# A sixth buffer for raw weight chunks in the two FFNs of a hybrid decoder layer

## Chip, cores and metric

One core of one Trainium2 chip runs the whole layer in one launch. The metric is the device time of one execution in microseconds (us), the median of several runs. The kernel before the change takes 1099.44 us (three runs, 1098.82 to 1101.89).

## The reference

One decoder layer over 512 tokens of width 1024, all in float32:

```python
D_MODEL, SEQ, D_FF = 1024, 512, 2816

def swiglu_ffn(x, g, w_gate, w_up, w_down):
    h = rms_norm(x, g)
    return (jax.nn.silu(h @ w_gate) * (h @ w_up)) @ w_down

x = x + 0.5 * swiglu_ffn(x, ffn1_norm, ffn1_w_gate, ffn1_w_up, ffn1_w_down)
h = rms_norm(x, mix_norm)
... = split_columns(h @ w_in)          # two attention branches, gates
x = x + merged @ w_out                 # the mixing stage
x = x + 0.5 * swiglu_ffn(x, ffn2_norm, ffn2_w_gate, ffn2_w_up, ffn2_w_down)
```

The change lies in the two FFNs. The mixing stage between them (a forgetting attention, a sparse attention with top-k keys, gates and an output projection) stays as it is.

## The kernel before

**Arithmetic.** Every float32 operand of a matrix product is split in two parts, high (rounded to the fast format F32R) and low (what the rounding left). A product is three matmuls: high by high, low by high, high by low (`mm3`, lines 141 to 143). Activations and weights are both split. For weights `split_w` does it: ScalarE casts the raw chunk to `wh` (line 112), and VectorE subtracts `wh` from the raw chunk to get `wl` (line 117). A few chunks have their low part made by a DMA that adds the raw chunk to minus `wh` (lines 114 and 115, issued from GpSimd). `wh` and `wl` have three buffers each.

**The FFN.** The 2816 hidden features are 22 blocks of 128. They are worked through in four groups (blocks 0 to 3, 4 to 9, 10 to 15, 16 to 21). In the first group each block is two plain steps, gate and up, each with one weight chunk of 128 x 1024 numbers (512 KB). In the other groups the blocks go in pairs, three pairs to a group, with a scheme of seven products of half size where a plain computation has eight (the code calls them A, S1, S2, B, S3, S4, D, and each is a step). A pair reads four raw chunks of 512 KB, called a, b, c and d, and forms from them with VectorE three running sums s1 = c + d (line 342), s2 = s1 + a (347), c = c + a (351) and later s2 = s2 + b (355). Products collect in PSUM banks pA, pB, pC and pD. The bank pB is used three times: for S2 and S3, then read by VectorE into `gu` (line 385), then for D. Each group ends with eight down steps, one chunk each, that add to x (line 421).

**The order of the work.** TensorE's order is written out by hand: the list `steps`. The other engines' instructions are placed by the framework's planner. It lays out the queue of each engine once, when the program is built, from a simulated timeline and the order of the code, and it may pull ready work ahead. On the chip every queue is worked through in order, SyncE's, which issues the loads, among them.

**Raw buffers.** A raw chunk sits in a buffer of 128 x 1024 numbers. The names `ra`, `rb` and `rc` belong to the kernel's weight pool and serve the mixing stage too. `re` belongs to each FFN's own pool. `rd` does as well, but holds a temporary (`xn`) during the plain steps and joins the others when the pairs begin. So five buffers serve the pairs. `load` (inside `ffn`, around line 460) takes the next chunk off a list and puts it in the free name that was used longest ago; a name never used comes first. `look_ahead(i)` is called before step i: it splits the weights of steps i to i + 2, loads what these need, marks the buffers free whose last reader it has written, and then loads for up to step i + 6 as long as a name is free. Buffers c and a of a pair are marked free with step S3, b with S4, d with D. A load's DMA waits on the chip until the last reader of the buffer's former content is through. While a pair runs, it holds four buffers, and one is left for the next pair.

Of the kernel before, what the change touches and what calls it, by code (L numbers as in the profile page):

```python
# [11 lines left out]
F32 = mybir.dt.float32  # L12
# [6 lines left out]
P = 128  # L19
# [32 lines left out]
def tile_hybrid_layer(ctx: ExitStack, tc: tile.TileContext, a: dict):  # L52
# [53 lines left out]
    def raw_tile(tag):  # L106
        return wpool.tile([P, 1024], F32, tag=tag, bufs=1, name=tag)
# [85 lines left out]
    def ffn(n, nxt, parts=lambda d: [slice(0, T)]):  # L193
        wg, wu, wp, wd = (a[f"w_{nm}{n}"] for nm in ("gate", "up", "pair", "down"))
        gi = 0 if n == 1 else 2
        with tc.tile_pool(name=f"ffn{n}", bufs=1) as ap, tc.tile_pool(name=f"halves{n}", bufs=1) as hp:
# [85 lines left out]
                    self.raw, self.loads, self.split, self.run, self.frees = raw, loads, split, run, frees  # L282
                    self.ahead = ahead

            free = {"ra", "rb", "rc", "re"}

            def plain(src, f, run, adding=False, ahead=2):
                raw = {}
# [173 lines left out]
            def load():  # L462
                i, (key, f, src) = queue.pop(0)

                tag = max(sorted(free), key=lambda z: used[::-1].index(z) if z in used else len(used))
                free.remove(tag)
                used.append(tag)
                t = ap.tile([P, 1024], F32, tag=tag, name=tag) if tag in ("rd", "re") else raw_tile(tag)
                steps[i].raw[key] = t, tag
                nc.sync.dma_start(t[:, :f * P].rearrange("p (n m) -> p n m", n=f) if f else t, src)  # L470

            def look_ahead(i):

                for j in range(i, min(i + 1 + steps[i].ahead, len(steps))):
                    if j not in ws:
                        while queue and queue[0][0] <= j:
                            load()
                        ws[j] = steps[j].split()
                        free.update(steps[j].raw[z][1] for z in steps[j].frees)
                while queue and queue[0][0] <= i + 6 and free:  # L480
                    load()
# [35 lines left out]
    gq = const.tile([P, 2], F32, name="gq")  # L517
    V.tensor_scalar(gq, hg[:, 0:2], -0.125, None, op0=OP.mult)
    ffn(1, lambda d, cols: (prep(d, 1), add_square(d)))


    with (tc.tile_pool(name="mix", bufs=1) as mp, ExitStack() as att_ctx,
# [247 lines left out]
        rb = next(norm)  # L770
# [313 lines left out]


    ffn(2, lambda d, cols: nc.sync.dma_start(a["y"][:, d, cols], x[d][:, cols]),
        lambda d: [slice(0, T)] if d < KD - 1 else [slice(0, T // 2), slice(T // 2, T)])

# [76 lines left out]
```

## Time and profile before

| what | value |
|---|---|
| median of 3 runs | 1099.44 us |
| the profiled execution | 1100.99 us |
| its span, first to last instruction | 1099.3 us |
| TensorE clock granted | 0.998 |
| moved by DMA | 127.86 MB |
| read from HBM | 104.94 MB |

The engines are PE (TensorE), PEld (its weight loads), DVE (VectorE), ACT (ScalarE), POOL (GpSimd) and SP (SyncE); a q behind the name is the engine's sequencer, which waits and issues DMAs. A row of a timeline gives start and duration in us, engine, line, operation, output and inputs by the program's names, sizes, count, and in brackets the idle time just before and what ended it. A row of a list of waits gives who waited for whom, then us in total, times, and the longest. A row of the stretches gives from and to, length, then the busy time of PE, PEld, DVE, ACT and POOL with counts, the granted clock, the share of the DMA engines, and GB/s. A row of DMA issues gives destination and source, queue, count, KB each, and the median us from issue to landing. All times of instructions are from the start of the span. Matmuls are pipelined and their ends are modelled.

### The profile page before, as it was taken

The numbers are of one execution on the slowest core, as the hardware profiler recorded it, in microseconds if no ns is written. First come the engines' busy times: TensorE is split into PE (matmuls) and PEld (weight loads), VectorE is DVE, ScalarE is ACT, GpSimd is POOL, SyncE is SP. The second block draws the span as 40 slices with busy tenths as digits, with TensorE's granted clock in tenths as the row PEclk, the third lists the DMA queues.
The fourth block names the chain that finished last, engine by engine and source line by source line (L and its number), as shares of the span: only waits on it lengthen the run. The fifth ranks groups of instructions, "written<-read, shape, count | busy, mean of one in ns | idle before, by whom it ended". The sixth has DMA issues, their size and how long they took to land.

```text
span 1099.3 us, 17737 instructions
## 1 busy us (share of the span) xinstructions
PE 1076.2 (98%) x6808; PEld 966.2 (88%) x6808; DVE 758.3 (69%) x1232; ACT 595.2 (54%) x970; POOL 200.9 (18%) x265
## 2 busy tenths in 40 slices
PE   8999999999999999999999999999999999999998
PEld 6889989998998889999878888788889989989997
DVE  5887666756767579987776665954877757655863
ACT  6636534743565575467766656534636625633551
POOL 1100000100000014357786662000100000100000
PEclk9999999999999999999999999999999999999999
DMA  7554443443442248733323321533544442533441
GB/s 220 137 152 119 111 118 104 110 132 100 113 124 79 96 125 183 191 118 97 87 58 98 124 77 49 163 98 103 116 150 115 125 126 81 134 103 110 126 108 75
DMA packets 45444, 127.86 MB, mean 116 GB/s; under 512 B 5544, under 2 KB 5928, under 8 KB 45360
## 3 DMA queue, kind: packets, MB, share of 16 engines
q1 hardware_dynamic: 38880, 110.22, 33.0%
q0 software_dynamic: 6336, 16.26, 8.3%
q8 instruction: 53, 0.87, 0.3%
q10 hardware_dynamic: 144, 0.26, 0.1%
q14 instruction: 31, 0.25, 0.1%
HBM read 104.94 MB, written 3.42 MB: 99 GB/s over the span
## 4 chain that ended last, share of the span: by engine, by line
PE 48%; DVE 7%; ACT 5%; POOL 3%; issue 2%; DMA 2%; DVEq 0%; POOLq 0%; ACTq 0%
PE pd L142 4%; PE pd L143 4%; PE pd L141 4%; PE ps_f L141 3%; PE ps_f L142 3%; PE ps_f L143 3%; PE ps_t L141 2%; PE ps_t L143 2%; PE ps_t L142 2%; PE pB L141 2%; PE pB L142 2%; PE pB L143 2%; PE ps_out L142 1%; PE pt L888 1%; PE ps_out L143 1%
## 5 line engine op out<-in xcount | busy, mean ns | idle before, releaser
L142 PE MATMUL pd<-al,wh 128*128 128x512 f32 (+1 forms) x358 | 138.3, 386 | 0.9 <-DVE al L217 0.9
L141 PE MATMUL pd<-ah,wh 128*128 128x512 f32 (+1 forms) x358 | 138.2, 386 | 0.0
L143 PE MATMUL pd<-ah,wl 128*128 128x512 f32 (+1 forms) x358 | 138.0, 386 | 0.0
L215 POOL DMA_DIRECT2D al<-gu x24 | 20.5, 856 | 500.0 <-ACT al L214 500.0
L112 ACT CAST wh<-s 128x1024 fp32r<-128x1024 f32 x54 | 56.8, 1052 | 82.9 <-PE pd L142 30.8
L117 DVE TENSOR_TENSOR wl<-s,wh 128x1024 fp32r<-128x1024 f32 x54 | 66.1, 1223 | 38.7 <-ACT wh L112 38.7
L421 DVE SCALAR_TENSOR_TENSOR x<-pd,x 128x512 f32<-128x512 f32 (+1 forms) x65 | 44.2, 681 | 67.9 <-PE pd L143 67.8
L141 PE MATMUL pB<-tbh,wh 128*128 128x256 f32 x288 | 81.4, 283 | 6.2 <-DVE gu L385 5.2
L141 PE MATMUL ps_t<-wh,xh 128*128 128x256 f32 (+1 forms) x288 | 80.7, 280 | 0.0
L142 PE MATMUL pB<-tbl,wh 128*128 128x256 f32 x288 | 80.4, 279 | 0.0
L143 PE MATMUL pB<-tbh,wl 128*128 128x256 f32 x288 | 80.4, 279 | 0.0
L142 PEld LDWEIGHTS pd<-al,wh 128*128 128x128 f32 x358 | 67.2, 188 | 14.9 <-DVE al L217 1.7
L142 PE MATMUL ps_t<-wl,xh 128*128 128x256 f32 (+1 forms) x288 | 80.3, 279 | 0.0
L143 PE MATMUL ps_t<-wh,xl 128*128 128x256 f32 (+1 forms) x288 | 80.3, 279 | 0.0
L141 PEld LDWEIGHTS pd<-ah,wh 128*128 128x128 f32 x358 | 67.2, 188 | 13.6 <-ACT ah L212 0.2
L143 PEld LDWEIGHTS pd<-ah,wl 128*128 128x128 f32 x358 | 67.3, 188 | 13.5
L141 PEld LDWEIGHTS pB<-tbh,wh 128*128 128x128 f32 x288 | 54.1, 188 | 8.3 <-issue 8.3
L141 PE MATMUL ps_f<-xh,wh 128*128 128x512 f32 x152 | 61.1, 402 | 0.0
L143 PE MATMUL ps_f<-xh,wl 128*128 128x512 f32 x152 | 60.4, 397 | 0.0
L142 PE MATMUL ps_f<-xl,wh 128*128 128x512 f32 x152 | 60.2, 396 | 0.0
L112 ACT CAST wh<-ra 128x1024 fp32r<-128x1024 f32 (+2 forms) x32 | 29.5, 923 | 50.4 <-PE pd L142 21.4
L112 ACT CAST wh<-re 128x1024 fp32r<-128x1024 f32 (+2 forms) x31 | 29.3, 946 | 48.7 <-PE pd L142 21.4
(332 smaller groups left out, 3486.6 us busy)
## 6 DMA issues: line engine op xcount, KB each, us to landing
rb<-in_w_pair_dram SPq DMA_DIRECT2D x16, 512.0 KB, 3.6
re<-in_w_pair_dram SPq DMA_DIRECT2D x16, 512.0 KB, 3.8
rd<-in_w_pair_dram SPq DMA_DIRECT2D x14, 512.0 KB, 3.7
rc<-in_w_pair_dram SPq DMA_DIRECT2D x13, 512.0 KB, 3.6
ra<-in_w_pair_dram SPq DMA_DIRECT2D x13, 512.0 KB, 3.6
al<-gu POOLq DMA_DIRECT2D x24, 256.0 KB, 3.9
rc<-in_w_down_dram SPq DMA_DIRECT2D x11, 384.0 KB, 3.1
ra<-in_w_down_dram SPq DMA_DIRECT2D x11, 384.0 KB, 3.2
```

Of the source, the lines that this page charges most:

```text
L112: S.copy(wh[:, :f], raw[:, :f])
L117: V.tensor_sub(wl[:, :f], raw[:, :f], wh[:, :f].bitcast(F32))
L141: PE.matmul(out, lh, rh, start=start, stop=False, **more)
L142: PE.matmul(out, lh, rl, start=False, stop=False, **more)
L143: PE.matmul(out, ll, rh, start=False, stop=stop, **more)
L215: G.dma_start(l, u, accum_op=OP.add)
L421: V.scalar_tensor_tensor(x[d][:, cols], ps, 0.5, x[d][:, cols], op0=OP.mult, op1=OP.add)
L888: PE.transpose(pt[:, i * P:(i + 1) * P], pr[i][:, j * P:(j + 1) * P], ident)
```

## The change

A sixth name, `rf`, is added to the set of free names in each FFN, and it gets a buffer of its own in that FFN's pool, just as `re` has. Nothing else is edited: the chunks, the sums, the products and TensorE's order are the same. The buffer adds 4 KB to each partition of the FFN's memory.

```diff
-            free = {"ra", "rb", "rc", "re"}
+            free = {"ra", "rb", "rc", "re", "rf"}
...
-                t = ap.tile([P, 1024], F32, tag=tag, name=tag) if tag in ("rd", "re") else raw_tile(tag)
+                t = ap.tile([P, 1024], F32, tag=tag, name=tag) if tag in ("rd", "re", "rf") else raw_tile(tag)
```

## The prediction

> **What bounds the kernel now.** I read the page first, then the busy time of four stretches, then who TensorE waits for, and last the instructions in order of time around one of those waits.
>
> ```profile
> PE 1076.2 (98%) x6808; PEld 966.2 (88%) x6808; DVE 758.3 (69%) x1232; ACT 595.2 (54%) x970; POOL 200.9 (18%) x265
> 0.00:60.00 60.00, 55.56 (x239) 44.39 (x240) 44.25 (x79) 38.19 (x59) 7.19 (x18) 1.00 0.63 172
> 60.00:360.00 300.00, 296.06 (x2039) 274.56 (x2038) 203.52 (x223) 150.34 (x205) 10.20 (x12) 1.00 0.42 116
> 360.00:760.00 400.00, 391.70 (x2320) 342.06 (x2320) 288.65 (x670) 244.65 (x486) 167.73 (x217) 1.00 0.39 111
> 760.00:1099.30 339.30, 332.90 (x2216) 305.18 (x2214) 221.88 (x263) 161.99 (x222) 15.77 (x18) 1.00 0.41 113
> ```
>
> TensorE sets the time: 1076.2 us of the 1099.3 us span, at clock 1.00 in all four rows. The change touches none of its instructions, so all that can be had is idle time of PE, 23.1 us. Of it 8.3 us (400 less 391.70) lie in the mixing stage, which the change doesn't touch. The DMA engines are used to about 0.4, so bandwidth is no bound after the first 60 us (0.63). Who does PE wait for?
>
> ```profile
> PE pB L141 <- DVE gu L385: 5.2, 11, 1.0
> PE pB L141 <- ACT wh L112: 1.0, 1, 1.0
> PE pd L142 <- DVE al L217: 0.9, 2, 0.7
> PE pu L143 <- DMA wl<-re: 0.4, 1, 0.4
> SPq L470 <- DVE wl L117: 521.4, 129, 10.7
> ```
>
> The last row looks like the prize, the loads waiting 521 us for buffers, but that is SyncE's queue, and SyncE has nothing else to do. What counts is on PE: no row there names a raw chunk. The largest is product D of a pair (pB, second use), which waits until VectorE has read product S3 out of the same bank (gu, L385). Why is VectorE late there? The first two pairs of the first group, VectorE and SyncE:
>
> ```profile
> 85.98 1.23 DVE L117 TENSOR_TENSOR wl<-rb,wh 128x1024 fp32r<-128x1024 f32 x1 [1.57 <-ACT wh L112]
> 88.83 1.23 DVE L117 TENSOR_TENSOR wl<-s,wh 128x1024 fp32r<-128x1024 f32 x1 [1.62 <-ACT wh L112]
> 90.88 1.23 DVE L342 TENSOR_TENSOR s<-rd,rb 128x1024 f32<-128x1024 f32 x1 [0.83 <-DMA rb<-in_w_pair_dram]
> 92.14 1.22 DVE L347 TENSOR_TENSOR s<-s,re 128x1024 f32<-128x1024 f32 x1
> 93.29 1.22 DVE L117 TENSOR_TENSOR wl<-rc,wh 128x1024 fp32r<-128x1024 f32 x1
> 94.42 1.22 DVE L351 TENSOR_TENSOR rd<-rd,re 128x1024 f32<-128x1024 f32 x1
> 95.56 0.68 DVE L385 SCALAR_TENSOR_TENSOR gu<-pB,p 128x512 f32<-128x512 f32 x1
> 111.65 1.23 DVE L342 TENSOR_TENSOR s<-ra,rd 128x1024 f32<-128x1024 f32 x1 [1.59 <-DMA rd<-in_w_pair_dram]
> 116.20 0.68 DVE L385 SCALAR_TENSOR_TENSOR gu<-pB,p 128x512 f32<-128x512 f32 x1
> 134.11 0.69 DVE L385 SCALAR_TENSOR_TENSOR gu<-pB,p 128x512 f32<-128x512 f32 x1 [0.60 <-PE pB L143]
> 84.44 0.33 SPq L470 DMA_DIRECT2D ra<-in_w_pair_dram  x1
> 87.23 0.33 SPq L470 DMA_DIRECT2D rb<-in_w_pair_dram  x1
> 107.32 0.33 SPq L470 DMA_DIRECT2D rd<-in_w_pair_dram  x1
> 96.39 0.36 PE L141 MATMUL pB<-tbh,wh 128*128 128x256 f32 x1 [0.21 <-DVE gu L385]
> 117.03 0.36 PE L141 MATMUL pB<-tbh,wh 128*128 128x256 f32 x1 [0.80 <-DVE gu L385]
> ```
>
> Read it backwards. PE stands 0.21 us until gu is done. gu is ready to go when S3 ends (the third pair shows it: there gu at 134.11 waits only for PE, and D waits for nothing), but VectorE is in order, and four instructions stand ahead of it, back to back from 90.88: the three sums for the next pair (L342, L347, L351) and one split. The first of them stood 0.83 us waiting for the next pair's chunk d in rb. That load was issued at 87.23, right as the split at 85.98 let go of rb, which held this pair's chunk c. Every link is there: buffer freed, load, sum, gu, PE. The second pair is the same with 1.59 us of waiting for rd and 0.80 us on PE. Twelve pairs have a pair right behind them (six groups of three), and twelve waits are in the two pB rows: 11 and 1.
>
> **The change part by part.** No instruction and no DMA is added or taken out: the same chunks go to other buffers. What moves are the loads and, as the planner lays out the queues anew, their places.
>
> (1) Which chunk gets which buffer. I played the choice (least recently used free name) through by hand for five and six names. With five, the second pair of a group takes c from the fifth buffer, d from the first pair's c, a from its a, b from its d; the rows above agree (rd and rb in L342, re in L347). With six, c and d both go to buffers that the previous pair doesn't hold, so both are on chip long before L342, and it is chunk a that waits for the first pair's c. So the late load doesn't vanish; it is still issued when the split at 85.98 ends, and lands about 90.8. But it now holds only L347 and L351. L342 can run in an earlier gap; VectorE has gaps of 1.57 and 1.62 us ahead of the splits at 85.98 and 88.83, and L342 takes 1.23.
>
> (2) What that gives gu. One instruction fewer stands between the landing and gu: 1.13 us (94.42 less 93.29, start to start). First pair: gu at 94.43 and done 0.68 later, 95.11; D could start at 96.39 less 0.21, 96.18. The wait goes. Second pair: gu ended at 116.88 and D started 0.15 later; 1.14 us sooner D is released at 115.89, and PE is ready at 116.23 (117.03 less 0.80). It goes with 0.34 us to spare. The worst one:
>
> ```profile
> 302.50 0.68 DVE L385 SCALAR_TENSOR_TENSOR gu<-pB,p 128x512 f32<-128x512 f32 x1
> 303.33 0.36 PE L141 MATMUL pB<-tbh,wh 128*128 128x256 f32 x1 [1.01 <-ACT wh L112]
> ```
>
> The row names ScalarE, but gu ends at 303.18, again 0.15 ahead of D, so this one belongs to gu as well. Released at 302.20 instead of 303.33, with PE ready at 302.32, it just goes. If all twelve go, the gain is 5.2 + 1.0 = 6.2 us; if L342 stays where it is, it fills the wait of 0.83 to 1.59 us, and gu still comes forward by about as much. Bounds: 6.2 us gained to nothing, and below nothing only if a split is held up (a rival). I take 6.2, since the spare time is positive in the smallest case. What is late next: D then starts as S4 ends, and nothing else in the pB rows is left.
>
> (3) The start of FFN 1. Here the new buffer changes the order of loads where the DMA engines are busiest.
>
> ```profile
> 20.41 0.33 SPq L470 DMA_DIRECT2D ra<-in_w_gate_dram  x1
> 22.15 0.33 SPq L470 DMA_DIRECT2D rb<-in_w_up_dram  x1
> 23.48 0.33 SPq L470 DMA_DIRECT2D re<-in_w_up_dram  x1
> DMA packets 599, 2.16 MB, mean 180 GB/s; under 512 B 64, under 2 KB 64, under 8 KB 597
> re<-in_w_up_dram SPq DMA_DIRECT2D x1, 512.0 KB, 7.8
> wl<-rc POOLq DMA_DIRECT2D x1, 512.0 KB, 8.2
> rb<-in_w_pair_dram SPq DMA_DIRECT2D x16, 512.0 KB, 3.6
> 31.41 1.05 ACT L112 CAST wh<-re 128x1024 fp32r<-128x1024 f32 x1 [9.33 <-DMA re<-in_w_up_dram]
> ```
>
> (The packets and the two single loads are of the stretch from 20 to 32 us.) Up chunk 2 in re takes 7.8 us against a usual 3.6, ScalarE stands 9.33 us for it, and the correction of its low half (wl<-re) comes 0.44 us too late for PE, the fourth row of PE's waits. After the change gate 3 goes to rf, issued behind re; up 3 takes ra, and the 256 KB chunk of the first down step takes rb. So re has 256 KB less ahead of it: at 180 GB/s about 1.4 us sooner, and the 0.44 goes. The other bound: if rf's 512 KB share the engines evenly with re, re lands up to 2.9 us later, and PE loses that on top. I take the gain of 0.4, since a load issued 0.4 us after another has no claim ahead of it.
>
> The Trainium skill speaks against this step: its page DMA: Bandwidth & Descriptors, section Issuing engines are not separate DMA queues, says that transfers run on the same 16 engines and interleave whoever issues them. By it, one more load in flight can only slow the other; the sum would be 3.3 us worse. The 8.2 us for wl<-rc beside a usual load's 3.6 shows such sharing between two queues; no row shows it within SyncE's.
>
> (4) The rest at nothing: eight down steps per group get their chunks one step earlier, but PE waits for none of them now; the memory of re and rf at the start of an FFN comes free with the stage before. The mixing stage's queues are laid out by the same planner and may shift by small amounts either way; its 8.3 us of idle could grow or shrink, which I bound by the scatter of the three runs, 1.5 us each way, and take as zero.
>
> **Sum.** 6.2 + 0.4 = 6.6 us. The profiled execution took 1100.99 us (its span of 1099.3 and 1.7 around it), so the same one would take 1094.4. It lies 1.55 above the median of the runs shown, 1099.44, from which I forecast 1092.8. A change of under 0.3%, 3.3 us, can't be told from none here, so faster means below 1096.1 and slower above 1102.7.
>
> **The rivals.** *A, the forecast*: L342 leaves the place in front of gu. For it: d's buffer is free a whole pair earlier, and the third pair shows that D doesn't wait when VectorE is clear. Its own range is 1091.3 (mixing stage 1.5 better) to 1096.1 (half the waits stay). Chance 0.67.
>
> *B, the wait is only handed on*: the last of three chunks lands at the same moment as now, since c's buffer frees at the same moment, and the planner fills the place that L342 leaves with the next split. The row for it stands at 93.30 on ScalarE:
>
> ```profile
> 93.30 1.06 ACT L112 CAST wh<-re 128x1024 fp32r<-128x1024 f32 x1 [1.26 <-PE pB L142]
> ```
>
> Its split could start at 94.36, so if it goes ahead of gu, gu is back at 95.56 and nothing is won: 1099.4, or about 1097.5 if half the pairs are like this. Against it: that cast itself waits for the end of S3, the very thing that makes gu ready, so in any timeline gu is ready 1.06 us sooner. Chance 0.22. On the Trainium skill's page Perfetto Trace Analysis, section Identifying Performance Opportunities, the rule is that gains generally come from the most contended engine. By it a buffer that leaves TensorE's work alone gives 1099.4; the twelve waits on that engine speak for more.
>
> *C, slower*: L342 now sits early in VectorE's queue, in front of splits that PE needs, and stands there for its DMA. Such a wait exists:
>
> ```profile
> 807.61 1.23 DVE L342 TENSOR_TENSOR s<-re,ra 128x1024 f32<-128x1024 f32 x1 [2.91 <-DMA ra<-in_w_pair_dram]
> 83.18 1.23 DVE L117 TENSOR_TENSOR wl<-ra,wh 128x1024 fp32r<-128x1024 f32 x1 [0.43 <-ACT wh L112]
> 87.85 0.28 PE L143 MATMUL pA<-b2h,wl 128*128 128x256 f32 x1
> ```
>
> The split at 83.18, chunk b's, ends at 84.41, and PE first reads what it wrote at 87.85, so the slack is 3.4 us. C decides only beyond that. If a chunk took 7.8 us as re did at the start, 4.2 more than usual, PE would lose 0.8 us at each of twelve places, 9.6, and gu would be as late as now, because c's split is held up too: 1109.0. Against it: c and d are issued most of a pair (20 us) ahead, and the longest such wait, 2.91 us, cost PE nothing. Chance 0.11.
>
> **The numbers.** Faster has A, 0.67; same has B, 0.22; slower has C, 0.11. The range runs from 1090.8 (A with 1.5 for the mixing stage and 0.5 for other waits of PE) to 1099.4, the whole of B; it leaves out C and little else.
>
> **What would show it.** Right: the two pB rows vanish from PE's waits or fall under 1 us; L342 no longer waits for a DMA but L347 does; gu starts within 1 us of S3's end in all 18 pairs; loads of SyncE name rf, with chunk a issued as c's split ends; wl<-re at 40 us is gone; PE's idle time falls from 23 to about 16.5 us, with the mixing stage still near 8.3. Wrong: gu still has four instructions ahead of it without a gap; VectorE stands for a DMA in front of a split; re lands later than at 31.4; or the mixing stage moves by more than 1.5 us.

## The result, and the profile after

The changed kernel takes 1091.03 us (median of four runs, 1090.42 to 1091.54); the kernel before takes 1099.46 us (four runs, 1098.82 to 1101.89). Between the medians lie 8.4 us. The ratio of the means is 0.9919, with a 95% interval of 0.9902 to 0.9936; that is 8.9 us. The forecast was 1092.8, a gain of 6.6 us, with a range down to 1090.8. The direction and the mechanism came out as forecast; the gain is larger, and by the means slightly more than the 8.6 us that the range allowed.

The profiled execution of the changed kernel took 1091.54 us. From its page the busy times, and then the same stretches as for the kernel before (the last one ends at 1089.0 us):

```profile
span 1089.8 us, 17737 instructions
PE 1071.7 (98%) x6808; PEld 964.2 (88%) x6808; DVE 761.1 (70%) x1232; ACT 594.5 (55%) x970; POOL 197.4 (18%) x265
```

```profile
0.00:60.00 60.00, 55.68 (x240) 44.70 (x241) 44.83 (x79) 38.73 (x59) 7.17 (x18) 0.97 0.64 177
60.00:360.00 300.00, 299.38 (x2085) 278.94 (x2084) 205.65 (x225) 151.38 (x206) 10.18 (x12) 1.00 0.40 116
360.00:760.00 400.00, 390.18 (x2301) 339.78 (x2300) 288.64 (x668) 246.06 (x486) 166.30 (x219) 1.00 0.37 111
760.00:1089.00 329.00, 326.44 (x2190) 300.73 (x2188) 222.01 (x262) 158.38 (x219) 13.78 (x16) 1.00 0.41 115
```

PE does the same 6808 instructions. In the stretch that holds FFN 1's pairs its idle time falls from 3.94 us (300 less 296.06) to 0.62 (300 less 299.38). That is 3.3 us, yet FFN 1's pairs and down steps became 4.7 us shorter. Over the whole span its idle time falls from 23.1 us (1099.3 less 1076.2) to 18.1 (1089.8 less 1071.7), 5 us for a gain of more than 8 (the forecast had 16.5 us left). That gap turns out to be the main lesson below.

The top of the list of who TensorE waits for (us in total, times, longest), and from further down what it still holds of the FFNs' down steps:

```profile
PE pg L453 <- ACT xh L152: 2.2, 2, 1.6
PE pt L888 <- POOL p L881: 2.1, 3, 1.0
...
PE pd L142 <- DVE al L217: 0.8, 2, 0.6
```

Both pB rows (5.2 and 1.0 us before) are gone altogether; what leads now are waits at the very start (pg) and in the mixing stage (pt). Of the splits of raw chunks (wl of line 117, wh of line 112) no row is left either in this profile. In a second profile of the same kernel (the ninth experiment) one is there, of 0.6 us, in a gate step (pg), as in the kernel before; no split of a pair is held up in either.

The same place as in the prediction, the first pair of FFN 1, on VectorE and on SyncE:

```profile
78.30 1.22 DVE L342 TENSOR_TENSOR s<-rc,rd 128x1024 f32<-128x1024 f32 x1
...
85.46 1.23 DVE L117 TENSOR_TENSOR wl<-re,wh 128x1024 fp32r<-128x1024 f32 x1 [1.57 <-ACT wh L112]
...
90.37 1.23 DVE L351 TENSOR_TENSOR rc<-rc,re 128x1024 f32<-128x1024 f32 x1 [0.82 <-DMA re<-in_w_pair_dram]
91.51 1.22 DVE L347 TENSOR_TENSOR s<-s,re 128x1024 f32<-128x1024 f32 x1
92.65 1.22 DVE L117 TENSOR_TENSOR wl<-rf,wh 128x1024 fp32r<-128x1024 f32 x1
93.78 0.68 DVE L385 SCALAR_TENSOR_TENSOR gu<-pB,p 128x512 f32<-128x512 f32 x1
```

```profile
86.72 0.33 SPq L470 DMA_DIRECT2D re<-in_w_pair_dram  x1
```

This pair's chunk c sits in re; its split ends at 86.69 (85.46 + 1.23), the load of the next pair's chunk a into re is issued at 86.72, and VectorE stands 0.82 us for it, as it stood 0.83 us for chunk d before. But now three instructions, not four, lie between the landing and gu: L342 ran 12 us earlier, at 78.30, in front of the pair. gu ends at 94.46, and D, which needs it, starts only after S4's last matmul. TensorE on both sides of that change-over:

```profile
95.38 0.28 PE L143 MATMUL pC<-b2h,wl 128*128 128x256 f32 x1
95.50 0.28 PE L141 MATMUL pB<-tbh,wh 128*128 128x256 f32 x1
```

D starts 1.04 us after gu's end, and 0.12 us after the matmul before it, like every other matmul of the row.

### The profile page after: what moved, and what is told of

It is laid out like the page before. It is cut to its first block, busy times and chain, and to the rows that moved or that the text cites. A ratio compares the mean times of both kernels' runs of the same rounds, so it can differ in the third digit from the quotient of the medians.

```text
span 1089.8 us, 17737 instructions
## 1 busy us (share of the span) xinstructions
PE 1071.7 (98%) x6808; PEld 964.2 (88%) x6808; DVE 761.1 (70%) x1232; ACT 594.5 (55%) x970; POOL 197.4 (18%) x265
## 4 chain that ended last, share of the span: by engine, by line
PE 50%; DVE 6%; POOL 3%; ACT 3%; issue 3%; DMA 1%; DVEq 0%; POOLq 0%; SPq 0%; ACTq 0%
PE pd L142 4%; PE pd L143 4%; PE pd L141 4%; PE ps_f L141 3%; PE ps_f L142 3%; PE ps_f L143 3%; PE pB L141 2%; PE pB L142 2%; PE pB L143 2%; PE pA L142 2%; PE pA L143 2%; PE pA L141 2%; PE ps_out L142 1%; PE ps_out L143 1%; PE ps_out L141 1%
## 5 line engine op out<-in xcount | busy, mean ns | idle before, releaser
L142 PEld LDWEIGHTS ps_t<-wl,xh 128*128 128x128 f32 x288 | 54.3, 188 | 0.5
L141 PEld LDWEIGHTS ps_t<-wh,xh 128*128 128x128 f32 x288 | 54.3, 189 | 0.5
```

What stands on the lines that cost most here:

```text
L141: PE.matmul(out, lh, rh, start=start, stop=False, **more)
L142: PE.matmul(out, lh, rl, start=False, stop=False, **more)
```

## The experiments

Theory: VectorE works its queue in order, the sums for the next pair stand ahead of the reading of pB, the first of them waits for a late load, and that is all that the sixth buffer cures. Rivals: the buffer matters for itself (more prefetch, so more buffers would win more), part of the gain comes from its other uses (plain steps, down steps, the start), or from the mixing stage being laid out anew. Times below are medians and ratios are of the means. "The two stretches" are FFN 1's pairs and down steps, from TensorE's first matmul into pA to its first of the mixing stage, and FFN 2's, from its first matmul into pA to TensorE's last instruction. Gains below are against the kernel before as it ran beside each group: 1100.94 us for the first four experiments, 1100.47 for the next four, 1099.92 for the last two.

**One FFN at a time.**

```diff
-            free = {"ra", "rb", "rc", "re", "rf"}
+            free = {"ra", "rb", "rc", "re", "rf"} if n == 1 else {"ra", "rb", "rc", "re"}
```

and the same with `n == 2`.

> The sixth buffer in the first FFN alone. Theory (the queue): the gain sits at the pairs that are followed by a pair, where the sum of chunks c and d no longer stands on VectorE between the late load and the reading of pB; by the order of TensorE's instructions in the two traces the first FFN's six places gave 4.7 us, the start 0.9, and the mixing stage, laid out anew, took 1.4. So 4.2 us under the kernel before, about 1095.2, with the second FFN's six waits for the reading of pB still there (some 3.0 us of idle time) and the mixing stage's loss of about 1.4 back again. Rival (loads in general): about half of 8.4 as well, but the second FFN no different. Rival (luck of the planner): no link to the FFN that has the buffer; the loss of the mixing stage need not come back.

> The sixth buffer in the second FFN alone. Theory: everything up to the end of the mixing stage is laid out as before, so the mixing stage loses nothing and the first FFN keeps its six waits (3.2 us of idle time); the second FFN's six places give 4.2 us: about 1095.2. If the mixing stage's 1.4 us came from the first FFN's new times, this kernel has them not. Rival (luck of the planner): any time between 1091 and 1099.

Measured: FFN 1 alone 1094.79 us, ratio 0.9945 (0.9931 to 0.9958); FFN 2 alone 1094.9, 0.9947 (0.9935 to 0.996). TensorE's waits for pB, FFN 1 alone and then FFN 2 alone:

```profile
PE pB L141 <- DVE gu L385: 2.5, 5, 0.9
PE pB L141 <- ACT wh L112: 2.2, 2, 1.1
```

```profile
PE pB L141 <- DVE gu L385: 3.2, 6, 1.6
```

With FFN 1 alone, FFN 2's six waits stay, and one of 0.51 us is left in FFN 1. It isn't the planner's doing: VectorE's instructions come in the same order there as in the full change, but at this place VectorE stood 2.43 us for chunk a instead of 1.60. With FFN 2 alone, FFN 1's six stay and FFN 2 has none. So the gain follows the FFN that has the buffer. The two gains, 6.2 and 6.0 us, add up to more than the 8.4 of both together, but with some 1.4 us of interval on each this is at the edge of what the runs can tell. In the profiled executions the two stretches together became 2.4 and 4.8 us shorter. The 2.4 is low because FFN 2's six waits were longer in that execution than in the kernel before (4.2 us listed instead of 3.0): the size of such a wait changes from one execution to the next.

**The same order with five buffers.** The kernel before, with the reading of pB put ahead of the three sums in VectorE's queue by hand:

```diff
+            def after_gu():
+                return tc.issue_after(read_b[0].ins) if read_b[0] else nullcontext()
...
-                    V.tensor_add(t["s1"], raw["c"][0], raw["d"][0])
+                    with after_gu():
+                        V.tensor_add(t["s1"], raw["c"][0], raw["d"][0])
...
-                    V.scalar_tensor_tensor(t["gu2"][:, :, HT:], view(t["B"]), -1.0, view(t["p5"]), op0=OP.mult, op1=OP.subtract)
+                    read_b[0] = V.scalar_tensor_tensor(t["gu2"][:, :, HT:], view(t["B"]), -1.0, view(t["p5"]), op0=OP.mult, op1=OP.subtract)
```

The sums of lines 347 and 351 are wrapped in the same way.

> Five buffers as before, but the three sums for the next pair are ordered behind the reading of pB on VectorE. Theory: the buffer matters only through what stands ahead of that reading, so all twelve waits vanish without it: 8.9 us less, 1090.6, and with 1.5 either way for the mixing stage 1089 to 1092; the start keeps its wait for the low half of up chunk 2. Rival (loads in general): the chunks land as late as before, so nothing is won: 1099.4.

Measured: 1090.23 us, 0.9904 (0.9891 to 0.9918): the whole gain, without the buffer. VectorE at the first pair (the kernel's lines lie 5 to 7 further down, so L392 is the reading of pB, L347, L353 and L358 are the three sums, and a split between them is left out):

```profile
93.12 0.69 DVE L392 SCALAR_TENSOR_TENSOR gu<-pB,p 128x512 f32<-128x512 f32 x1 [0.61 <-PE pB L143]
93.73 1.22 DVE L347 TENSOR_TENSOR s<-rd,rb 128x1024 f32<-128x1024 f32 x1
...
96.00 1.22 DVE L353 TENSOR_TENSOR s<-s,re 128x1024 f32<-128x1024 f32 x1
97.14 1.22 DVE L358 TENSOR_TENSOR rd<-rd,re 128x1024 f32<-128x1024 f32 x1
```

Now gu itself waits for PE (0.61 us, the end of S3), and the sums come behind it. In all 18 pairs gu starts as S3 ends and is done 1.9 us before D. No pB row is left. This is the run that decides between the order and the buffer.

**The sixth buffer everywhere but in the pairs.** Pair chunks (`f` is 0 for them) may not take rf; plain and down steps may:

```diff
-                tag = max(sorted(free), key=lambda z: used[::-1].index(z) if z in used else len(used))
+                tag = max(sorted(free if f else free - {"rf"}), key=lambda z: used[::-1].index(z) if z in used else len(used))
...
-                while queue and queue[0][0] <= i + 6 and free:
+                while queue and queue[0][0] <= i + 6 and (free if queue[0][1][1] else free - {"rf"}):
```

> Six buffers, but the sixth may only hold chunks of the plain and the down steps, none of a pair's. Theory: the twelve waits at the reading of pB stay (about 6 us of idle time), only the start's 0.9 us is won: about 1098.5, with 1.5 either way for the mixing stage. Rival (loads in general): the plain and down steps have 46 of the 82 loads of the first FFN's and as many of the second's steps, so half of the gain of 8.4 should stay: about 1095.

The text on record miscounts: 38 of FFN 1's 74 loads and 40 of FFN 2's 76 may use rf, not 46 of 82. Measured: 1101.29 us, 1.0003 (0.9995 to 1.0012). Nothing is gained in all. TensorE's waits for pB:

```profile
PE pB L141 <- DVE gu L385: 4.6, 9, 1.6
PE pB L141 <- ACT wh L112: 3.2, 3, 1.1
```

All twelve are there. The rival's 1095 is out: the interval leaves a gain of some 0.5 us at most. But by itself this run doesn't show that the other uses bring nothing. The waits for pB are longer here (7.8 us listed, 6.2 before), and the two stretches took 1.6 us more in its profile than before, so up to some 2 us could be won elsewhere and lost again here. For the down steps the third and the eighth experiment close this: the two stretches took 274.40 and 274.51 us in both, with five buffers and with six. The start is taken up by the last two experiments, the mixing stage further down.

**A seventh buffer, and one fewer.** The set of free names with `rg` as well, which gets a buffer as `rf` has, and the kernel before with `re` taken out.

```diff
-            free = {"ra", "rb", "rc", "re", "rf"}
+            free = {"ra", "rb", "rc", "re", "rf", "rg"}
```

```diff
-            free = {"ra", "rb", "rc", "re"}
+            free = {"ra", "rb", "rc"}
```

> A seventh buffer beside the sixth, so that chunks c, d and a of the next pair are all loaded early. Theory: VectorE no longer waits for a chunk at the second sum (L347), and the reading of pB starts at S3's end, but D was already on time with six buffers, so TensorE has nothing left to win in the pairs: as with six, 1091, with 1.5 either way for the mixing stage. Rival (loads in general): each further buffer brings the loads forward again and wins some microseconds more, 1087 or less.

> One buffer fewer than before, four for the pairs. Theory: while a pair runs, no buffer is left for the next; chunk c of the next pair then takes this pair's c, and its load starts at the very moment at which chunk d's starts with five. So the sum c + d stands where it stood and TensorE's waits for the reading of pB stay near 6 us; what is new are waits for chunks where down steps and pairs meet and in the plain steps. Time 1099 to 1106. Rival (loads in general): the waits at the reading of pB grow by a landing each, twelve times a microsecond or more, beyond 1110.

Measured: seven buffers 1091.65 us, 0.9904 (0.9889 to 0.9919), not to be told from six; four buffers 1099.68 us, 0.9994 (0.9984 to 1.0004), no worse than five. With seven, gu is done 1.9 us before D in every pair. In the traces that makes the two stretches 0.4 us shorter than with six, where D is still a little late at three places (next section); it is nothing that the medians can tell. Once D is not late, an earlier gu is worth nothing. With four, the first pair on VectorE and SyncE:

```profile
90.39 1.23 DVE L342 TENSOR_TENSOR s<-rb,rd 128x1024 f32<-128x1024 f32 x1 [0.85 <-DMA rb<-in_w_pair_dram]
91.65 1.23 DVE L347 TENSOR_TENSOR s<-s,ra 128x1024 f32<-128x1024 f32 x1
92.80 1.22 DVE L117 TENSOR_TENSOR wl<-rc,wh 128x1024 fp32r<-128x1024 f32 x1
93.93 1.22 DVE L351 TENSOR_TENSOR rb<-rb,ra 128x1024 f32<-128x1024 f32 x1
95.07 0.68 DVE L385 SCALAR_TENSOR_TENSOR gu<-pB,p 128x512 f32<-128x512 f32 x1
```

```profile
86.72 0.33 SPq L470 DMA_DIRECT2D rb<-in_w_pair_dram  x1
```

The same four instructions stand ahead of gu, behind a wait of nearly the same length (0.85 us, with five buffers 0.83), for a load issued as c's split ends. The new waits for chunks that the text on record expected don't show: TensorE's list names no load. Four and five buffers have the same late load; the sixth is the first that moves L342 out from behind it.

**gu held back in the changed kernel.** Six buffers, and two copies of pB that the layer doesn't need ahead of gu, so that it is late again by design:

```diff
+                    for _ in range(2):
+                        V.tensor_copy(view(tmp_tile("late")), view(t["B"]))
                     V.scalar_tensor_tensor(t["gu2"][:, :, HT:], view(t["B"]), -1.0, view(t["p5"]), op0=OP.mult, op1=OP.subtract)
```

> Six buffers, and two copies of pB into a scratch tile put ahead of the reading of pB, in all 18 pairs (they do work that the layer doesn't need). They hold the reading up by about 1.2 us. D's start after the reading's end has these margins in the six-buffer trace, less the 0.15 us that the release takes: 0.89, 0.49, 0.69, 0.17, 1.05, 0, 0.03, 0, 1.08, 0.47, 1.05, 0.41, and 1.76 in the third pairs. So TensorE's start of D slips by 1.2 less each of these, 8.1 us over twelve places. Theory (a wait costs 0.16 us more than the idle time shown, and 0.07 to get going): the list of waits shows about 6.1 us, the time rises by 8.9, to 1100. Rival (the idle time shown is the price): the time rises by what the list shows, 6.1, to 1097.

Measured: 1100.56 us, 0.9995 (0.9985 to 1.0004). The whole gain is lost, with all buffers and loads in place. VectorE and then TensorE's waits:

```profile
93.28 1.28 DVE L386 COPY late<-pB 128x512 f32<-128x512 f32 x2
94.48 0.68 DVE L387 SCALAR_TENSOR_TENSOR gu<-pB,p 128x512 f32<-128x512 f32 x1
```

```profile
PE pB L141 <- DVE gu L387: 3.4, 6, 0.9
PE pB L141 <- ACT wh L112: 3.0, 3, 1.1
```

gu comes 1.2 us later. The list shows 6.4 us of waits; the two stretches became 9.8 us longer than in the changed kernel. So a listed wait is worth more than its listed length, here as in the change.

**Six buffers and the order by hand.** The edit of the third experiment on top of the change.

> Six buffers and the three sums ordered behind the reading of pB. Theory: no wait for that reading is left by either means, so the two don't add up: the time of five buffers with the sums behind (0.9904 of before), less about 0.9 us at the start of the first FFN, 0.9896 of before, with 1.5 us either way for the mixing stage. Rival (loads in general): the gains add up, 0.983 of before.

Measured: 1089.62 us, 0.9896 (0.9883 to 0.9909). It has the lowest median of all, but its interval overlaps those of the order alone (0.9891 to 0.9918) and of the buffer alone (0.9902 to 0.9936), so the two cures don't add up.

**The changed kernel once more, and without rf in the plain steps.** The second bars rf from the chunks of the plain steps, so that the loads at the start go to the buffers they had before:

```diff
-                tag = max(sorted(free), key=lambda z: used[::-1].index(z) if z in used else len(used))
+                tag = max(sorted(free if f != KD else free - {"rf"}), key=lambda z: used[::-1].index(z) if z in used else len(used))
```

The condition of the loop in `look_ahead` gets the same guard.

> The changed kernel as it is, on the same chip and between the same runs of before as the next kernel. Open are two terms outside the pairs. The mixing stage: if the layout of its queues costs 1.3 us, the wait of 0.7 us for GpSimd ahead of a transposition, 472 us into the span, is there again; if it was that one execution, it is not, and the mixing stage equals before's. The start: the half-clock stretch of that execution hid whether the low half of up chunk 2 comes in time; with the clock full before 40 us, the theory (one load of 256 KB less ahead of it) has no wait there, the rival (it is a matter of how the loads happen to share the engines) has one of up to 0.5 us. Time 0.990 to 0.993 of before.

> Six buffers, but the sixth may not hold chunks of the plain steps, only of down steps and pairs. The theory puts all but a few tenths of the gain into the pairs: no wait for the reading of pB, the time within 0.5 us of six buffers throughout, which a comparison of two medians can't tell from nothing; the wait for the low half of up chunk 2 is back, 0.4 us, if the clock is full there. Rival (loads in general): the plain steps and the early fetch of the down steps carry a share, so some microseconds are lost.

Measured: the changed kernel 1091.7 us, 0.9917 (0.9903 to 0.9932); without rf in the plain steps 1092.3, 0.9929 (0.9916 to 0.9942). The two can't be told apart. TensorE's wait at the start in the first, and then the same wait and what is left at pB in the second:

```profile
PE pu L143 <- DMA wl<-re: 0.6, 1, 0.6
```

```profile
PE pu L143 <- DMA wl<-re: 0.7, 1, 0.7
PE pB L141 <- DVE gu L385: 0.3, 1, 0.3
```

The wait that the change should have removed at the start is there again in the first of them, which is the changed kernel itself.

## Why the prediction was right in its mechanism, and which term failed

**Which buffer gets which chunk (step 1): right, but for one detail.** Before, VectorE waited for the late load at L342 in all twelve places. After, L342 waits only where a group begins, but for one wait of 0.49 us at 812 us, and it is chunk a that comes late in the twelve places, as forecast. The forecast had L347 wait for it; that holds in the six second pairs. In the six first pairs the planner put L351 ahead of L347, and L351 waits, as in the rows above.

**gu comes forward (step 2): right in mechanism and place.** The forecast let gu end 1.07 us before D could start in the first pair (95.11 against 96.18); measured 1.04. It gave the second pair 0.49 us (0.34 to spare, with the 0.15 from gu's end to D), and 0.64 was measured. But it took D's earliest start from the drawn end of the matmul ahead, which the next paragraph shows to be 0.16 us too late; without that it had 0.9 and 0.3 us, so the closeness in the first pair is partly luck. Of the wait at 303 us it said that "it just goes", with 0.12 us to spare by the same drawn end. In the changed kernel the same pair comes 5.2 us sooner, and D starts 0.15 us behind gu's end (297.97), the distance of a matmul that was just released:

```profile
297.29 0.68 DVE L385 SCALAR_TENSOR_TENSOR gu<-pB,p 128x512 f32<-128x512 f32 x1
297.92 0.28 PE L143 MATMUL pC<-b2h,wl 128*128 128x256 f32 x1
298.12 0.35 PE L141 MATMUL pB<-tbh,wh 128*128 128x256 f32 x1
298.32 0.28 PE L142 MATMUL pB<-tbl,wh 128*128 128x256 f32 x1
```

No wait is listed in these rows, but D starts 0.20 us behind the matmul ahead of it instead of 0.12, and the next one 0.20 behind D: D is still a little late. The same is seen at 828 and 848 us. The three places cost 0.39 us together: the two stretches took 274.57 and 274.73 us here, and 274.40 and 274.51 in each of the three kernels in which no gu is late (the third, fifth and eighth experiment). Across the twelve pairs gu ends 0.15 to 1.23 us before D starts. So the statement that gu would start within 1 us of S3's end in all 18 pairs was wrong: that holds in ten (an undelayed gu ends 1.91 us before D; in eight pairs less than 0.91 is left). Six buffers cure the wait with thin margins; the order by hand cures it with 1.91 everywhere.

**What the twelve waits are worth (the sum of step 2): this is the term that failed.** The prediction took a wait to cost the idle time listed for it, and added up 5.2 + 1.0 = 6.2 us. TensorE in the kernel before, at the first of them:

```profile
95.90 0.28 PE L143 MATMUL pC<-b2h,wl 128*128 128x256 f32 x1
96.39 0.36 PE L141 MATMUL pB<-tbh,wh 128*128 128x256 f32 x1 [0.21 <-DVE gu L385]
96.58 0.28 PE L142 MATMUL pB<-tbl,wh 128*128 128x256 f32 x1
```

Matmuls of this shape start every 0.117 us when they flow, but each is drawn 0.28 us long, since its end is modelled. Idle time is counted from the drawn end. D started 0.49 us after its forerunner instead of 0.117: 0.37 us late, of which 0.16 (0.28 less 0.117) lie hidden under the drawn length and 0.21 are listed. The matmul after it then starts 0.19 later instead of 0.12: 0.07 more. Twelve times 0.16 is 2.0, twelve times 0.07 is 0.8, and 6.2 + 2.0 + 0.8 = 9.0 us. Measured, FFN 1's stretch of pairs and down steps went from 279.26 to 274.57 us and FFN 2's from 279.06 to 274.73. That is 4.69 + 4.33 = 9.02 us where the prediction had 6.2. That it meets 9.0 to 0.02 is partly luck, since 0.39 us of the waits is left. Against the kernels in which no gu is late, the kernel before takes 9.41 us more (4.86 and 4.55); about 0.4 us of that lies at other steps, a few hundredths each, and isn't explained. The seventh experiment shows the same the other way round: 6.4 us listed, 9.8 us lost, where the corrected price would be 9.2.

On the Trainium skill's page Perfetto Trace Analysis, section Tensor Engine Instruction, it says that the profiler estimates a matmul's end from its size, so its time is a model and not a measurement. The rows agree: 0.28 us drawn where the next one starts after 0.12.

**The start (step 3): not shown.** The forecast let up chunk 2, in re, land 1.4 us sooner and a wait of 0.4 us go. The two single loads and ScalarE's cast of re in the changed kernel's profile:

```profile
re<-in_w_up_dram SPq DMA_DIRECT2D x1, 512.0 KB, 6.9
rf<-in_w_gate_dram SPq DMA_DIRECT2D x1, 512.0 KB, 9.3
```

```profile
30.91 1.05 ACT L112 CAST wh<-re 128x1024 fp32r<-128x1024 f32 x1 [7.58 <-DMA re<-in_w_up_dram]
```

re took 6.9 us instead of 7.8, and the wait is absent. But in the repeat of the same kernel re took 8.0 us, the cast began at 31.34 (31.41 before), and TensorE waited 0.6 us. So the new order of the loads didn't bring re in by 1.4 us, and didn't push it back by up to 2.9 either; a gain of 0.4 can't be claimed. What decides whether this wait appears wasn't settled: it is there in three of the ten experiments and in the kernel before. The 0.9 us that some expectations grant the start come from that one profile too: from TensorE's first matmul into pg behind line 180 (at 26.92 us before, 27.35 after) to the first pair it took 52.29 us before and 51.35 after, but 52.44 in the repeat. As for the prediction's 8.2 us of wl<-rc beside a load's 3.6, these are two kinds of transfer; others of wl's kind take from 4.5 us in the same trace, so they make a weaker case for sharing than it seemed.

**The mixing stage (step 4): zero was right.** TensorE's idle time there went from 8.3 to 9.8 us in the profile (400 less 390.18), 1.52 more and so just over the bound of 1.5. In the repeat it is 8.85 (400 less 391.15). Part of it is one row, which the repeat doesn't have:

```profile
472.20 0.66 PE L888 MATMUL pt<-ident,p 128*128 128x128 f32 x4 [0.72 <-POOL p L881]
```

It is one execution's, not the layout's: the stage wasn't laid out anew at all. From FFN 1's last matmul to FFN 2's first, TensorE, VectorE, ScalarE and GpSimd have the same instructions in the same order in the traces before and after (2284, 666, 483 and 217 of them); only SyncE's loads for the start of FFN 2 differ. So the rival that part of the gain comes from a new layout of this stage is out. The changed kernel's profile got through the stage only 0.2 us sooner than the one of before, though the latter lost some 1.5 us there to a spell of halved clock (last section).

**The rivals.** B, that the wait is only handed on, had one thing right: the last of three chunks lands at the same moment as before, and a split does stand ahead of gu (92.65 in the timeline above). It was as far ahead of gu before, and no new one took L342's place. (The prediction's second time for B, 1097.5 with half the pairs held up, doesn't follow from its sum: half of 6.6 us gives 1096.1.) C, a split held up behind L342: the longest wait of L342 after the change is 2.6 us, below the slack of 3.4 us, and no split of a pair shows in TensorE's waits. On the Trainium skill's page Perfetto Trace Analysis, section Identifying Performance Opportunities, the rule is that gains generally come from the most contended engine. The prediction read it as no change for a buffer that leaves TensorE's work alone; by the runs the gain lies in that engine's waits, though none of its instructions changed, so the reading was too narrow and the rule isn't contradicted.

**The sum.** The profiled executions differ by 9.45 us where the prediction's sum was 6.6: pairs 9.02 for 6.2, the time up to the first pair 0.51 for 0.4 (by luck: the repeat reaches the first pair only 0.07 us sooner than the kernel before), the mixing stage and FFN 2's start together 0.06 worse for nothing. The range from 1090.8 allowed 0.5 us for waits of PE beyond the forecast; the mis-sized price was 2.8.

## What to carry to other kernels

Follow a wait of the busiest engine back through the in-order queue of the engine that it waits for: what stands ahead of the late instruction there, and what that waits for, is the cause, and a further buffer is only one way to move it; putting the urgent instruction first did the same here with no memory. Price a wait on TensorE by the spacing of matmul starts, not by the listed idle time: each of the twelve cost 0.23 us more than its row said, and 0.27 by the kernels in which none is left, about half as much again. Another queue's large number (SyncE's 521 us of waiting for buffers, 494 after the change) is no prize when nothing waits for that queue.

## What the runs showed of the hardware that was not expected

In seven of the twelve profiles the granted clock drops to one half for a stretch of 3.4 us, in one of them twice, and in five not at all, the last microseconds of a span left aside. The places are few: 10.8 us in the changed kernel, 24.0 to 25.3 in the second, third, fifth and sixth experiment, and 434.9 to 440.6 in the kernel before and the fifth and seventh. The stretch in the kernel before, and the one ahead of it:

```profile
437.20:440.60 3.40, 3.40 (x28) 3.23 (x27) 3.37 (x10) 3.05 (x6) 2.24 (x2) 1.00 0.54 110
440.60:444.10 3.50, 3.50 (x10) 2.73 (x9) 3.50 (x14) 0.00 (x0) 1.65 (x3) 0.51 0.81 167
```

And in the changed kernel:

```profile
7.40:10.80 3.40, 1.77 (x6) 1.13 (x7) 1.55 (x2) 2.39 (x4) 0.00 (x0) 1.00 1.03 395
10.80:14.20 3.40, 3.40 (x9) 2.36 (x9) 3.37 (x6) 3.40 (x7) 0.00 (x0) 0.50 1.00 321
```

Columns as in the other stretches; the third from the right is the granted clock. Matmuls of 512 columns start every 0.43 us in it instead of 0.23, and TensorE is about 1.5 us later behind it where it has work throughout. What precedes it is little work on the array: in the changed kernel PE is busy 1.77 us of 3.40, at 24 to 25 us 2.2, and in the kernel before the stretch ahead holds twenty matmuls of 8 columns (line 811) that are drawn as busy. All profiles pass the same places, and only some of them drop there. On the Trainium skill's page TensorE: Matmul & The Clock Gate, section What's actually happening, a monitor halves the clock after an idle window of some 3.4 us, and the windows run freely, without regard to the kernel's start. The length agrees, and so does it that the drop comes in some executions and not in others; but the window ahead wasn't idle here, it held half a window's work or many small matmuls. No experiment tested the cause. It goes along with part of the scatter between runs of one kernel: of the kernel before beside the fifth to eighth experiment, ten runs with a clock of 1.0 took 1099.7 us in the mean, and six with 0.997 took 1101.5. And it can make one stage differ between two profiles with no edit behind it: in the eight experiments without such a stretch there, TensorE went from FFN 1's end to FFN 2's start 1.2 to 1.8 us faster than in the kernel before; in the two with one there, it took 0.1 to 0.2 us longer.
